# Strassen's seven products for part of the FFN down projection, woven between gate and up chunks

## The chip, the cores and the metric

The kernel runs on one core of a Trainium2 chip. The metric is the device time of one execution in microseconds. A core has a matrix engine (TensorE: PE in the profile, its weight loads PEld), VectorE (DVE), ScalarE (ACT), GpSimd (POOL) and SyncE (SP, which issues most DMAs here). The engines run side by side, each works through its own list in order, and they wait for each other by semaphores. PE multiplies a stationary block of 128x128 with a moving block of 128 rows and up to 512 columns into a bank of the accumulator memory (PSUM); DVE and ACT carry the sums out of it.

## What is computed

Two decoder layers over 512 tokens of width 1024, all in float32. Layer 0 mixes tokens by sliding-window attention, layer 1 by a chunked spatial gating unit (SGU). Each ends with the FFN that the change touches:

```
def swiglu(h, w_gate_up, w_down):
    gu = h @ w_gate_up                                   # 1024 -> 2 x 2816
    return (silu(gu[..., :2816]) * gu[..., 2816:]) @ w_down   # 2816 -> 1024
...
h = rmsnorm(x, norm_ffn_pre[i])
x = x + rmsnorm(swiglu(h, ...), norm_ffn_post[i])
```

## The kernel before

**Precision by three products.** Every float32 operand is split into a high part that the matrix engine takes at full rate (float32r, hi) and the rest (lo). `mm3` (line 210) issues hi·hi, hi·lo and lo·hi, so each block of a projection costs three matmuls. Activations are split once, where they are made; weights are split as they stream in.

**Weight stream.** All weights lie in HBM in the order of use, in chunks of eight 128x128 blocks (512 KB). `fetch` (223) issues the load of a chunk into one of `NRAW` = 2 raw buffers through SyncE's queue. `split` (238) makes the chunk ready: ACT copies raw to the high tile `wh` (257), DVE subtracts to the low tile `wl` (253). High and low tiles come from one pool of `NW` = 17 tiles of 128x1024; rows of gains and biases (`row_tile`) take tiles of it too. A chunk gives its two tiles back when its last use is issued.

**Order by a planner.** The lists of PE, DVE and ACT are written out when the program is built. A planner keeps a modelled time `now` for PE and busy times for DVE and ACT; `Side` objects are generators of follow-up steps with due times (softmax, evacuations, norms). `tick` (155) runs what is due and otherwise asks `split_idle` (262) whether the next chunk should be split: at once if its slack is below a stage's bound (`PLAN`), else only if ACT and DVE are free and no step marked as a chain is due soon.

**FFN before (609).** The 22 slices of 128 hidden columns go in two halves of 11 (`HJ`). A half makes gate and up for its slices: per slice two PSUM banks, eight k blocks, 48 matmuls of 512 columns and two chunks. The first three slices of the first half run by token halves with 256 columns, because tokens 2 and 3 are not normalised yet. `evac_gu` (610) takes a slice out: ACT's Silu (614), DVE's product with the up half (620), ACT's high part (624), DVE's low part (627). The half's down projection then runs over its 11 slices: for each of the two column halves and four token blocks, `tok_mm` (590) adds three matmuls of 512 columns per slice. The first half's sums are copied to tiles `m` by ACT (678); the second half's are added to them by DVE (689) and start each token's norm (`Tok`, 488). In the last FFN the last token's second column half runs as two of 256 columns, and its results are written out (567).

**Around it.** Attention comes before the first FFN, SGU before the second. At each boundary the weights of the next stage are split ahead as far as `NW` tiles allow, while DVE and ACT run the norm of the tokens.

Of the kernel before, what the change touches and what calls it, by code (L numbers as in the profile page):

```python
# [6 lines left out]
F32 = mybir.dt.float32  # L7
# [13 lines left out]
HJ = NJ // 2  # L21
# [4 lines left out]
NW = 17  # L26
# [5 lines left out]
NRAW = 2  # L32
# [16 lines left out]

V0 = 0  # L50
# [5 lines left out]
SV0 = GU0 + 3 * NJ * KT  # L56
# [5 lines left out]
NBLK = GU1 + 3 * NJ * KT  # L62

def uses(i):

    if i < Q0 or WO0 <= i < GU0 or SO0 <= i < GU1:
        return 4
    if SV0 <= i < SO0:  # L70
        return 4 if i < SU0 or SV1 <= i < SU1 else 2 if i < SV1 else 1
    if i < WO0:
        return 1
    b = i - GU0 if i < SV0 else i - GU1
    f, b = divmod(b, 3 * HJ * KT)
    if b >= 2 * HJ * KT:
        return 4
    return 2 if f == 0 and b < 3 * 2 * KT else 1
# [3 lines left out]
def trunk_kernel(ctx, tc, x_t, xt, w, cols, rows, ws_t, consts, out):  # L82
# [136 lines left out]
    left = [0] * NCH  # L219
    for i in range(NBLK):  # L220
        left[i // CB] += uses(i)

    def fetch(free=0.0, most=NBLK):
        while len(raws) < min(NCH, len(chunks) + NRAW, most):
            c = len(raws)
            if c == NLATE:
                load_x()
            if c == NLATE + 1:
                nc.sync.dma_start(c_msk[:, 0:256], consts[:, 1024:1280])
                nc.sync.dma_start(c_msk[:, 256:384], consts[:, 1408:1536])  # L230
                nc.sync.dma_start(cs[:], consts[:, 0:1024])
                busy["d"] += 2.5
            raw = rawp.tile([P, CB * P], F32, tag="raw", name=nm("raw"))
            nc.sync.dma_start(raw[:], w[c])
            busy["d"] = max(busy["d"], now[0], free) + 1.46
            raws[c] = (raw, busy["d"] + DLAT)

    def split():
        c = len(chunks)
        fetch()  # L240
        raw, ready = raws[c]
        assert used[0] + 2 <= NW
        used[0] += 2
        wh = wp.tile([P, CB * P], F32R, tag="w", name=nm("wh"))
        wl = wp.tile([P, CB * P], F32R, tag="w", name=nm("wl"))

        def low(f):
            yield f
            if c in POOL_LOW:
                nc.gpsimd.tensor_tensor(wl[:], raw[:], wh[:].bitcast(F32), ALU.subtract)  # L250
                chunks[c][3] = f + 2.4
            else:
                nc.vector.tensor_tensor(wl[:], raw[:], wh[:].bitcast(F32), ALU.subtract)  # L253
                chunks[c][3] = V(CB * P, f)
            fetch(chunks[c][3])

        nc.scalar.activation(wh[:], raw[:], AF.Copy)  # L257
# [52 lines left out]
    def drop(n=1):  # L310
        used[0] -= n

# [296 lines left out]
    def ffn(base, nx_in, g1o, nx_out):  # L609
# [30 lines left out]

        h = hsrc(nx_in)

        def gu(g, b0, j, hf):
            grab("acc")
            grab("acc")
            ps = (acc(), acc())
            for k in range(KT):
                rh, rl = h(k, hf)
                for u in range(2):
                    wh, wl = blk(b0 + (j * KT + k) * 2 + u)  # L650
                    mm3(ps[u][:, hf], wh, wl, rh, rl, k == 0, k == KT - 1)
                tick()
            evac_gu(g, j, *ps, hf)

        m = None
        for f in range(2):
            stage[0] = (2 if base == GU0 else 6) + f
            b0 = base + f * (HJ * KT * 3)
            ga = [gp.tile([P, 8, S], F32R, tag="ga", name=nm("ga")) for _ in range(2)]
            gb = [gp.tile([P, 3, S], F32R, tag="gb", name=nm("gb")) for _ in range(2)]  # L660
            g = [[ga[i][:, k] if k < 8 else gb[i][:, k - 8] for k in range(HJ)] for i in range(2)] + [{}]
            j0 = 0
            if f == 0:
                pace[0] = 2.5
                for hf in halves:
                    for j in range(3):
                        gu(g, b0, j, hf)
                j0 = 3
            pace[0] = 5.1
            for j in range(j0, HJ):  # L670
                gu(g, b0, j, full)
            d0 = b0 + HJ * KT * 2
            l = gsrc(g)
            if f == 0:
                m = new_m()
                for c in range(2):
                    def evac0(t, ps):
                        nc.scalar.activation(m[t][c][:], ps[:], AF.Copy)
                        A(S, now[0] + 0.2)
                    tok_proj(d0 + c * HJ * 4, HJ, l, evac0)  # L680
                continue
# [10 lines left out]
            tok_proj(d0, HJ, l, lambda t, ps: add(t, 0, ps), False)  # L692
            hold[0] = now[0] + NB * HJ * 0.65
            for t in range(NB if nx_out is not None else NB - 1):
                grab("acc")
                ps = acc()
                for k in range(HJ):
                    tok_mm(ps, l, t, k, d0 + HJ * 4 + 4 * k, k == 0, k == HJ - 1)
                add(t, 1, ps)
            if nx_out is None:  # L700
                t = NB - 1
                until(lambda: toks[0].done)
                for i, hf in enumerate(halves):
                    grab("acc")
                    ps = acc()[:, 0:256]
                    for k in range(HJ):
                        lh, ll = l(k, slice(t * P, (t + 1) * P))
                        wh, wl = blk(d0 + HJ * 4 + 4 * k, 4 if i else 0, 4)
                        mm3(ps, lh, ll, wh[:, hf], wl[:, hf], k == 0, k == HJ - 1)
# [3 lines left out]
            drop()  # L713


    def attention(nx_in, g1o, nx_out):
# [263 lines left out]
        hold[0] = now[0] + NB * 8 * 0.65 + 10  # L980
        for t in range(NB):
            tok = Tok(t, m[t], g1, nx_out)
            for c in range(2):
# [7 lines left out]
        drop(2)  # L991


    def sgu(nx_in, g1o, nx_out):
# [157 lines left out]
        drop()  # L1152
# [73 lines left out]
def _layout(inputs):  # L1226
# [30 lines left out]
    def ffn(i):  # L1257
        gu = blocks(a["ffn_w_gate_up"][i]).reshape(KT, 2, NJ, P, P)
        dn = blocks(a["ffn_w_down"][i])
        for h in range(2):  # L1260
            js = slice(h * HJ, (h + 1) * HJ)
            seq.append(gu[:, :, js].transpose(2, 0, 1, 3, 4).reshape(-1, P, P))
            for c in range(2):
                seq.append(flat(dn[js][:, 4 * c:4 * c + 4]))
# [12 lines left out]
    assert w.shape[0] == NBLK  # L1277
    w = np.ascontiguousarray(w.reshape(NBLK // CB, CB, P, P).transpose(0, 2, 1, 3).reshape(NBLK // CB, P, CB * P))

# [40 lines left out]
```

## Time and profile before

| | |
|---|---|
| median of 3 runs | 1066.5 us (1066.02 to 1067.13) |
| the profiled execution | 1067.36 us |
| its span, first to last instruction | 1065.6 us |
| PE busy | 1046.0 us, 98% |
| DVE busy | 524.8 us, 49% |
| ACT busy | 438.4 us, 41% |
| moved by DMA | 105.10 MB, 99 GB/s over the span |
| mean granted clock of PE | 0.994 |

The profiled execution lies 1.8 us above its own span. PE's ends are modelled in this profile, so its busy time overlaps from one matmul to the next; the distance from start to start tells the rate, and the wait for another engine tells a stall.

### The profile page before, as it was taken

Reading aid. Unit: us, or ns where it says so; the run is one execution under the profiler, and the core shown is the slowest. Engines: PE = TensorE matmul, PEld = TensorE weight load, DVE = VectorE, ACT = ScalarE, POOL = GpSimd, SP = SyncE. Lnnn points to the kernel's source line nnn. Section 1 sums busy time; section 2 is a strip of 40 time slices with the busy share of each in tenths; the row PEclk is TensorE's granted clock in tenths of the full one; section 3 lists DMA queues with packets and bytes.
Section 4 is the critical chain, followed back from the end, with each engine's and each line's share of the span. In section 5 each row is a group of like instructions: output and inputs, shape, how many; then the busy total and the mean of one; then the engine's idle time right before and its main releaser. Section 6 shows DMA issues by size and latency. Waiting matters only on the chain.

```text
span 1065.6 us, 13311 instructions
## 1 busy us (share of the span) xinstructions
PE 1046.0 (98%) x5237; PEld 869.6 (82%) x5237; DVE 524.8 (49%) x1074; ACT 438.4 (41%) x775; POOL 24.2 (2%) x22
## 2 busy tenths in 40 slices
PE   7998998999999999999999999999999999999997
PEld 6875666988888888888889888899888888888886
DVE  6699679743332233332474867584333223333335
ACT  4799676632322223222255444573223222232210
POOL 2000002000000000000000000100000000000000
PEclk9999999999999999999999999999999999999999
DMA  8322101433233322223133233034223332222302
GB/s 292 125 93 80 60 21 60 131 127 99 99 99 99 99 99 95 94 92 135 59 119 100 79 125 106 28 120 151 90 97 98 99 99 99 99 99 98 101 1 80
DMA packets 29839, 105.10 MB, mean 99 GB/s; under 512 B 3344, under 2 KB 3872, under 8 KB 29776
## 3 DMA queue, kind: packets, MB, share of 16 engines
q1 hardware_dynamic: 29088, 103.10, 29.1%
q8 instruction: 41, 0.67, 0.3%
q10 hardware_dynamic: 576, 0.92, 0.2%
q0 software_dynamic: 112, 0.23, 0.2%
q14 instruction: 22, 0.18, 0.0%
HBM read 102.13 MB, written 2.10 MB: 98 GB/s over the span
## 4 chain that ended last, share of the span: by engine, by line
PE 88%; DVE 7%; ACT 2%; DMA 1%; issue 1%; POOL 0%; DVEq 0%; ACTq 0%; POOLq 0%
PE acc L204 86%; DVE wl L253 1%; DVE p L828 1%; ACT rt L746 1%; PE aux L459 1%; DVE p L859 1%; DMA raw<-w 1%; PE acc L888 1%; DMA c_cols<-cols 1%; PE aux L896 0%; DVE rt L740 0%; ACT wh L257 0%; ACT p L850 0%; DVE hl L1168 0%; PE aux L457 0%
## 5 line engine op out<-in xcount | busy, mean ns | idle before, releaser
L253 DVE TENSOR_TENSOR wl<-raw,wh 128x1024 fp32r<-128x1024 f32 x174 | 214.5, 1234 | 413.0 <-PE acc L204 340.4
L204 PE MATMUL acc<-hh,wh 128*128 128x512 f32 (+1 forms) x960 | 352.1, 367 | 0.0
L204 PE MATMUL acc<-hl,wh 128*128 128x512 f32 (+1 forms) x960 | 349.8, 364 | 0.0
L204 PE MATMUL acc<-hh,wl 128*128 128x512 f32 (+1 forms) x960 | 349.7, 364 | 0.0
L257 ACT ACTIVATE wh<-raw 128x1024 fp32r<-128x1024 f32 x176 | 185.8, 1058 | 220.4 <-PE acc L204 184.6
L204 PE MATMUL acc<-wh,ga 128*128 128x512 f32 (+1 forms) x736 | 236.2, 392 | 2.7 <-DVE ga L915 2.7
L204 PEld LDWEIGHTS acc<-hh,wh 128*128 128x128 f32 x960 | 181.0, 188 | 29.1 <-issue 0.2
L204 PEld LDWEIGHTS acc<-hh,wl 128*128 128x128 f32 x960 | 180.9, 188 | 28.9
L204 PEld LDWEIGHTS acc<-hl,wh 128*128 128x128 f32 x960 | 181.0, 189 | 28.8 <-issue 0.2
L204 PEld LDWEIGHTS acc<-wh,ga 128*128 128x128 f32 x736 | 138.3, 189 | 35.1 <-issue 4.9
L204 PE MATMUL acc<-wl,ga 128*128 128x512 f32 (+1 forms) x368 | 142.3, 387 | 0.0
L614 ACT ACTIVATE t<-acc 128x512 f32<-128x512 f32 (+1 forms) x50 | 27.3, 545 | 146.5 <-PE acc L204 146.5
L204 PEld LDWEIGHTS acc<-wl,ga 128*128 128x128 f32 x368 | 69.8, 190 | 12.8
L204 PE MATMUL acc<-wh,gb 128*128 128x512 f32 (+1 forms) x198 | 61.9, 383 | 0.0
L624 ACT ACTIVATE ga<-t 128x512 fp32r<-128x512 f32 (+1 forms) x38 | 21.5, 565 | 53.5 <-DVE t L620 53.4
L204 PEld LDWEIGHTS acc<-wh,gb 128*128 128x128 f32 x198 | 36.9, 188 | 7.2
L503 POOL TENSOR_TENSOR m<-m,row 128x512 f32<-128x512 f32 x12 | 17.2, 1433 | 1020.6 <-ACT acc L381 1020.6
L204 PE MATMUL acc<-wh,hh 128*128 128x512 f32 (+1 forms) x96 | 34.4, 368 | 4.4 <-ACT wh L257 4.4
L204 PE MATMUL acc<-wl,gb 128*128 128x512 f32 (+1 forms) x99 | 37.9, 383 | 0.0
L381 ACT ACTIVATE acc<-m 128x512 f32<-128x512 f32 x30 | 18.0, 598 | 46.5 <-DVE m L689 42.1
L204 PE MATMUL acc<-wh,hl 128*128 128x512 f32 (+1 forms) x96 | 34.3, 367 | 0.7 <-DVE hl L1168 0.7
L627 DVE TENSOR_TENSOR ga<-t,ga 128x512 fp32r<-128x512 f32 (+1 forms) x38 | 23.1, 607 | 21.1 <-ACT ga L624 21.1
(124 smaller groups left out, 830.4 us busy)
## 6 DMA issues: line engine op xcount, KB each, us to landing
raw<-w SPq DMA_DIRECT2D x176, 512.0 KB, 3.5
row<-rows SPq DMA_DIRECT2D x8, 512.0 KB, 4.5
xg<-xt SPq DMA_DIRECT2D x4, 512.0 KB, 7.3
x<-x_t SPq DMA_DIRECT2D x4, 512.0 KB, 7.3
out<-x SPq DMA_DIRECT2D x4, 256.0 KB, 2.1
out<-x ACTq DMA_DIRECT2D x3, 256.0 KB, 2.1
cs<-consts SPq DMA_DIRECT2D x1, 512.0 KB, 7.2
t<-ws_t SPq DMA_DIRECT2D x2, 256.0 KB, 4.3
```

What stands on the lines that cost most here:

```text
L204: nc.tensor.matmul(ps, a, b, start=start, stop=stop)
L253: nc.vector.tensor_tensor(wl[:], raw[:], wh[:].bitcast(F32), ALU.subtract)
L257: nc.scalar.activation(wh[:], raw[:], AF.Copy)
L381: nc.scalar.activation(junk, src, AF.Square, accum_out=s[:, c:c + 1])
L459: nc.tensor.transpose(dst, self.src[t][k // 4][:, (k % 4) * P:(k % 4 + 1) * P], ident)
L503: nc.gpsimd.tensor_tensor(self.m[c][:], self.m[c][:], self.g1[:, cols2[c]], ALU.mult)
L614: nc.scalar.activation(t1[:, hf], pg[:, hf], AF.Silu)
L624: nc.scalar.activation(g[0][jj][:, hf], t1[:, hf], AF.Copy)
L627: nc.vector.tensor_tensor(g[1][jj][:, hf], t1[:, hf], g[0][jj][:, hf].bitcast(F32), ALU.subtract)
L746: nc.scalar.activation(ro[o:o + 32, hf], t1[q * 32:q * 32 + 32, hf], AF.Identity, bias=b[q * 32:q * 32 + 32])
L828: nc.vector.tensor_tensor_reduce(pt[:, 2 * g2 + g, i, 0:nk], sc[i][:, g * 256:g * 256 + nk], mask[:, 256 - nk:256], 0.125, sink_bc[:, pr * ...
L859: nc.vector.tensor_scalar(p(j), p(j), sm[:, j:j + 1], None, ALU.mult)
```

## The change

The down projection of the first 12 of the 22 slices (`AJ`) is no longer done as a plain product. Its operand is cut into token halves (two of 256), slices of a pair (even and odd) and column halves (two of 512), which makes it a 2x2 by 2x2 block product, and that is done by Strassen's seven products instead of eight. Each product sums over three groups of four slices (`NQ`) and keeps two PSUM banks; `settle` copies or adds its sums into the tiles `m`, 24 times in all per FFN.

The left operand of a product is a sum or difference of two blocks of the activations (five of seven products) or one block (two of seven), made by DVE and then split by ACT and DVE into a ring of two (`operands`). The right one is a sum or difference of two weight chunks (again five of seven): both are loaded, DVE adds or subtracts one into the other, then the sum is split as any chunk. A chunk of weights is loaded and split anew for each product that takes it.

The first 12 slices' gate and up come first, with their activations kept unsplit in float32 (`evac_raw`: Silu and product only). Then 21 product steps (7 products, 3 groups, 12 matmuls each) and 20 half slices of gate and up of the other ten slices (24 matmuls each) alternate: one half slice, two product steps, then one and one. The plain down projection of those ten slices ends the FFN as before. Besides: `NW` falls from 17 to 15, `NRAW` rises from 2 to 4, and a gain row's tile counts as free only when the tokens have used it (`drop_after`).

```
-NW = 17
+NW = 15
-NRAW = 2
+NRAW = 4
+AJ = 12
+BJ = NJ - AJ
+NQ = AJ // 4
...
+PRODUCTS = (
+    (((0, 0), (1, 1), 1), ((0, 0), (1, 1), 1)),
+    (((1, 0), (0, 0), -1), ((0, 0), (0, 1), 1)),
+    (((1, 1), None, 0), ((1, 0), (0, 0), -1)),
+    (((0, 1), (1, 1), -1), ((1, 0), (1, 1), 1)),
+    (((0, 0), None, 0), ((0, 1), (1, 1), -1)),
+    (((0, 0), (0, 1), 1), ((1, 1), None, 0)),
+    (((1, 0), (1, 1), 1), ((0, 0), None, 0)),
+)
...
     def fetch(free=0.0, most=NBLK):
-        while len(raws) < min(NCH, len(chunks) + NRAW, most):
+        while len(raws) < min(NCH, most) and raw_used[0] + len(STREAM[len(raws)][0]) <= NRAW:
...
+        if len(tiles) == 2:
+            op = ALU.add if STREAM[c][1] > 0 else ALU.subtract
+            nc.vector.tensor_tensor(raw[:], raw[:], tiles[1][:], op)
+            f = V(CB * P, ready)
+            raw_used[0] -= 1
+            fetch(f)
+            chunks[c] = [wh, wl, None, None, f]
+            chunks[c][2] = Side(high_low(f), f)
+            return
...
-        slack = max(now[0], hold[0]) + (c - cur[0] - 1) * pace[0] - max(now[0], busy["v"], busy["a"]) - 2.4
+        slack = max(now[0], hold[0]) + (c - cur[0] - 1) * pace[0] - max(now[0], busy["v"], busy["a"]) - (2.4 if len(STREAM[c][0]) == 1 else 3.7)
...
+                if y is not None:
+                    yield from take("t")
+                    t = tmp()[:].rearrange("p (a t) -> p a t", a=2)
+                    nc.vector.tensor_tensor(t, src, view(y), ALU.add if sign > 0 else ALU.subtract)
+                    src = t
+                    f = V(S, now[0])
+                    yield f
+                hi, lo = (r.rearrange("p (a t) -> p a t", a=2) for r in ring[n % 2])
+                nc.scalar.activation(hi, src, AF.Copy)
+                f = A(S, f)
+                yield f
+                nc.vector.tensor_tensor(lo, src, hi.bitcast(F32), ALU.subtract)
...
+        Side(operands(), now[0], True)
+        pace[0] = 4.0
...
+        def settle(p, ps):
+            for sign, th, c in TARGETS[p]:
+                for i in range(2):
+                    d = m[2 * th + i][c][:]
+                    if sign == "=":
+                        nc.scalar.activation(d, ps[i][:], AF.Copy)
+                        A(S, now[0] + 0.2)
+                    else:
+                        nc.vector.tensor_tensor(d, d, ps[i][:], ALU.add if sign == "+" else ALU.subtract)
+                        V(S, now[0] + 0.2)
+
+        for kind, a, b in ITEMS:
+            if kind == "g":
+                if b == 0:
+                    gps = two()
+                gu(gps, at - b * CB, range(4 * b, 4 * b + 4), full)
+                if b:
+                    evac_gu(g, a - AJ, *gps, full)
+            else:
+                if b == 0:
+                    banks = two()
+                until(lambda: (a, b) in made)
+                f, hi, lo = made[a, b]
+                wait(f)
+                for kp in range(2):
+                    for i in range(2):
+                        ts = slice(i * P, i * P + P)
+                        wh, wl = blk(at + 4 * kp, 4)
+                        mm3(banks[i][:], hi[:, kp, ts], lo[:, kp, ts], wh, wl,
+                            b + kp == 0, b == NQ - 1 and kp == 1)
+                        tick()
+                spent[0] += 1
+                if b == NQ - 1:
+                    settle(a, banks)
```

## Rows read from the trace of the kernel before

**Rows 1.** The page's first part: the span, and each engine's busy us, share and instructions.

```profile
span 1065.6 us, 13311 instructions
PE 1046.0 (98%) x5237; PEld 869.6 (82%) x5237; DVE 524.8 (49%) x1074; ACT 438.4 (41%) x775; POOL 24.2 (2%) x22
```

**Rows 2.** What PE waited for over the whole span: all rows of that view (engine, line, releaser: us in total, times, longest us).

```profile
PE acc L204 <- ACT wh L257: 4.4, 1, 4.4
PE aux L896 <- ACT t L900: 3.6, 3, 2.4
PE acc L204 <- DVE ga L915: 2.7, 1, 2.7
PE acc L172 <- DVE zero L164: 1.1, 1, 1.1
PE acc L204 <- DVE hl L1168: 0.7, 1, 0.7
```

**Rows 3.** The chain that ended last, in order of time (start us, us, what): its two longest pieces, one in each FFN.

```profile
205.46 336.82 PE acc L204 x1548
...
714.43 344.14 PE acc L204 x1617
```

**Rows 4.** The list of PE's instructions in order of time (start us, us shown, line, operation): matmuls of 512 columns in a row, in the first half's gate and up and then in its down projection; then, at the start of the first FFN, matmuls of 256 columns.

```profile
300.04 0.39 PE L204 MATMUL acc<-hh,wh 128*128 128x512 f32 x1
300.27 0.39 PE L204 MATMUL acc<-hl,wh 128*128 128x512 f32 x1
...
302.31 0.39 PE L204 MATMUL acc<-hl,wh 128*128 128x512 f32 x1
...
329.74 0.39 PE L204 MATMUL acc<-wh,ga 128*128 128x512 f32 x1
329.96 0.39 PE L204 MATMUL acc<-wh,gb 128*128 128x512 f32 x1
...
183.09 0.28 PE L204 MATMUL acc<-hh,wh 128*128 128x256 f32 x1
...
183.67 0.28 PE L204 MATMUL acc<-hh,wl 128*128 128x256 f32 x1
```

**Rows 5.** Busy time by stretch of 20 us: the stretch, its length, then busy us (instructions) of PE, PEld, DVE, ACT, POOL, then PE's granted clock, the DMA share and GB/s. Attention (60:80, 80:100), its end and the first FFN's start (160:180), the first FFN's gate and up (440:460), SGU (600:620), the second FFN's start (720:740).

```profile
60.00:80.00 20.00, 20.00 (x121) 14.94 (x120) 19.48 (x62) 19.16 (x51) 0.00 (x0) 1.00 0.25 79
80.00:100.00 20.00, 18.02 (x101) 12.30 (x99) 18.86 (x58) 19.76 (x42) 0.00 (x0) 1.00 0.23 80
...
160.00:180.00 20.00, 17.33 (x78) 12.41 (x77) 19.53 (x55) 11.22 (x25) 5.49 (x4) 0.91 0.17 54
...
440.00:460.00 20.00, 20.00 (x90) 16.57 (x89) 6.28 (x8) 5.46 (x8) 0.00 (x0) 1.00 0.32 106
...
600.00:620.00 20.00, 20.00 (x90) 16.57 (x89) 19.40 (x45) 8.78 (x13) 0.00 (x0) 1.00 0.16 53
...
720.00:740.00 20.00, 20.00 (x136) 18.54 (x135) 9.63 (x12) 8.42 (x12) 0.00 (x0) 1.00 0.49 163
```

**Rows 6.** Groups of instructions by line with different shapes kept apart (line, engine, operation, names, shapes, count | busy us, mean ns of one | idle us of the engine before them and who ended it).

```profile
L253 DVE TENSOR_TENSOR wl<-raw,wh 128x1024 fp32r<-128x1024 f32 x174 | 214.5, 1234 | 413.0 <-PE acc L204 340.4 <-ACT wh L257 72.3
L257 ACT ACTIVATE wh<-raw 128x1024 fp32r<-128x1024 f32 x176 | 185.8, 1058 | 220.4 <-PE acc L204 184.6 <-DMA raw<-w 35.6
...
L620 DVE TENSOR_TENSOR t<-t,acc 128x512 f32<-128x512 f32 x38 | 25.8, 680 | 0.0
...
L614 ACT ACTIVATE t<-acc 128x512 f32<-128x512 f32 x38 | 22.8, 599 | 142.0 <-PE acc L204 142.0
...
L627 DVE TENSOR_TENSOR ga<-t,ga 128x512 fp32r<-128x512 f32 x26 | 18.0, 693 | 18.2 <-ACT ga L624 18.2
...
L624 ACT ACTIVATE ga<-t 128x512 fp32r<-128x512 f32 x26 | 16.5, 633 | 45.1 <-DVE t L620 45.1
...
L689 DVE TENSOR_TENSOR m<-acc,m 128x512 f32<-128x512 f32 x15 | 10.0, 688 | 24.3 <-PE acc L204 24.3
L678 ACT ACTIVATE m<-acc 128x512 f32<-128x512 f32 x16 | 9.6, 598 | 15.7 <-PE acc L204 14.7
...
L751 DVE TENSOR_TENSOR rt<-rt,cs 128x512 f32<-128x512 f32 x10 | 6.8, 685 | 0.0
```

**Rows 7.** The page's last part, the loads of weights: queue, count, KB each, median us from issue to landing.

```profile
raw<-w SPq DMA_DIRECT2D x176, 512.0 KB, 3.5
```

**Rows 8.** Who waited for whom on SyncE's queue in the first 60 us, and ACT's list in the same stretch: the wait of the third chunk's split for its load.

```profile
SPq L234 <- POOL wl L250: 8.0, 2, 6.4
...
17.57 1.06 ACT L257 ACTIVATE wh<-raw 128x1024 fp32r<-128x1024 f32 x1 [3.12 <-DMA raw<-w]
```

**Rows 9.** DVE's list in order of time at the three stage boundaries: the third chunk of the first FFN; the last chunks split before the second FFN and the next; token 1's last add before SGU and the low part of the last of its activation blocks.

```profile
177.92 1.22 DVE L253 TENSOR_TENSOR wl<-raw,wh 128x1024 fp32r<-128x1024 f32 x1
...
665.84 1.23 DVE L253 TENSOR_TENSOR wl<-raw,wh 128x1024 fp32r<-128x1024 f32 x1 [0.26 <-ACT wh L257]
697.03 1.23 DVE L253 TENSOR_TENSOR wl<-raw,wh 128x1024 fp32r<-128x1024 f32 x1 [1.21 <-ACT wh L257]
...
532.80 0.69 DVE L689 TENSOR_TENSOR m<-acc,m 128x512 f32<-128x512 f32 x1 [2.70 <-PE acc L204]
...
551.49 0.87 DVE L476 SCALAR_TENSOR_TENSOR hl<-aux,c_cols,hh 128x256 fp32r<-128x256 f32 x2
```

More of the change, by code (lines that the diff above doesn't have):

```diff
@@ L20 @@
 NJ = FF // P
-HJ = NJ // 2
 EPS = 1e-6
@@ L48, with _items, _stream, plain @@
 GROUPS = ((0,), (1,), (2, 3))
+PRODUCTS = (
[7 rows of a table added]
+)
+TARGETS = (
+    (("=", 0, 0), ("=", 1, 1)),
+    (("+", 1, 1),),
+    (("=", 1, 0), ("+", 0, 0)),
+    (("+", 0, 0),),
+    (("=", 0, 1), ("+", 1, 1)),
+    (("+", 0, 1), ("-", 0, 0)),
+    (("+", 1, 0), ("-", 1, 1)),
+)
+def _items():
+    ps = [("p", p, q) for p in range(len(PRODUCTS)) for q in range(NQ)]
+    gs = [("g", AJ + j, half) for j in range(BJ) for half in range(2)]
+    n, out = len(ps) + len(gs), []
+    while ps or gs:
+        if gs and (not ps or len(gs) * (n - len(gs)) >= len(ps) * len(gs) and len(gs) >= len(ps) * BJ * 2 / (7 * NQ)):
+            out.append(gs.pop(0))
+        else:
+            out.append(ps.pop(0))
+    return out
+ITEMS = _items()
+def _stream():
+    st, n = [], [0]
+    def plain(blocks, uses):
+        for _ in range(blocks // CB):
+            st.append(((n[0],), 0, uses))
+            n[0] += 1
+    def ffn():
+        plain(3 * 2 * KT, 2)
+        plain((AJ - 3) * 2 * KT, 1)
+        gb = n[0]
+        qb = gb + 2 * BJ
+        for kind, a, b in ITEMS:
+            if kind == "g":
+                st.append(((gb + 2 * (a - AJ) + b,), 0, 1))
+            else:
+                x, y, sign = PRODUCTS[a][1]
+                at = lambda z: qb + 4 * b + 2 * z[0] + z[1]
+                st.append(((at(x),) if y is None else (at(x), at(y)), sign, 2))
+        n[0] = qb + 4 * NQ
+        plain(2 * BJ * 4, 4)
+    plain(16, 4)
+    plain(80, 1)
+    plain(64, 4)
+    ffn()
+    plain(32, 4)
+    plain(16, 2)
+    plain(32, 4)
+    plain(48, 1)
+    plain(64, 4)
+    ffn()
+    return st, n[0]
+STREAM, NHBM = _stream()
 V0 = 0
@@ L232, in fetch @@
                 busy["d"] += 2.5
[L233 to L236, printed above, removed]
+            tiles = []
+            for b in reversed(STREAM[c][0]):
+                raw = rawp.tile([P, CB * P], F32, tag="raw", name=nm("raw"))
+                nc.sync.dma_start(raw[:], w[b])
+                busy["d"] = max(busy["d"], now[0], free) + 1.46
+                tiles.insert(0, raw)
+            raw_used[0] += len(tiles)
+            raws[c] = (tiles, busy["d"] + DLAT)
     def split():
@@ L240, in split @@
         fetch()
-        raw, ready = raws[c]
+        tiles, ready = raws[c]
+        raw = tiles[0]
         assert used[0] + 2 <= NW
@@ L311, in drop, with drop_after, side @@
         used[0] -= n
+    def drop_after(toks):
+        def side():
+            while any(len(t.half) < 2 for t in toks):
+                yield now[0] + 0.2
+            drop()
+        Side(side(), now[0])
     xs = [xp.tile([P, D], F32, tag=f"x{k}", name=f"x{k}") for k in range(NB)]
@@ L644, in gu, with two @@
+        h = hsrc(nx_in)
+        def gu(ps, b, js, hf):
+            for k in js:
+                rh, rl = h(k, hf)
+                for u in range(2):
+                    wh, wl = blk(b + 2 * k + u)
+                    mm3(ps[u][:, hf], wh, wl, rh, rl, k == 0, k == KT - 1)
+                tick()
+        def two():
             grab("acc")
             grab("acc")
[L646 to L678, printed above, removed]
-                        A(S, now[0] + 0.2)
-                    tok_proj(d0 + c * HJ * 4, HJ, l, evac0)
-                continue
+            return acc(), acc()
@@ new lines, in pair_tile @@
+        def pair_tile(dt=F32):
+            grab("rt")
+            return tp.tile([P, 2, S], dt, tag="rt", name=nm("rt"), bufs=3)
+        stage[0] = 2 if base == GU0 else 6
+        pace[0] = 2.5
+        for hf in halves:
+            for j in range(3):
+                ps = two()
+                gu(ps, base + j * 2 * KT, range(KT), hf)
+                evac_raw(raw_g(j), j, *ps, hf, raw_ready)
+        pace[0] = 5.1
+        for j in range(3, AJ):
+            if j == 8:
+                rt += [pair_tile(), pair_tile()]
+            ps = two()
+            gu(ps, base + j * 2 * KT, range(KT), full)
+            evac_raw(raw_g(j), j, *ps, full, raw_ready)
@@ L682, in ffn @@
+        for _ in range(3):
+            give("rt")
+        pace[0] = 5.1
+        stage[0] += 1
+        d0 = at
+        l = gsrc(g)
+        if 1:
             spare[0] = 0
@@ L1151, in sgu @@
             evac(t, 1, ps)
-        drop()
+        drop_after(toks)
+        for _ in range(NY):
+            give("rt")
     n0, n1, n2, n3 = (NextH(i) for i in range(4))
```

123 lines of the change are left out of this document (89 added, 34 removed).

## Prediction

> **What bounds the kernel now.** I read the page's engine table first: PE is busy in 98% of the span, DVE in 49%, ACT in 41% [rows 1]. Because PE's ends are modelled, I then asked what PE waited for: five waits in the whole span, 12.5 us together, all on lines of the start and of attention and none on a line of the FFN [rows 2]. The chain that ended last says the same: one piece of matmuls runs for 336.8 us through the first FFN and one for 344.1 us through the second [rows 3]. The last question is the rate. Ten matmuls of 512 columns start between 300.04 and 302.31, so 0.227 us from one to the next, and the rows of the down projection show the same step [rows 4]. A stretch of 20 us at granted clock 1.00 holds about 90 of them, in gate and up with DVE at 6.28 us and in SGU with DVE at 19.40 us alike [rows 5]. So in the FFN the time is the number of matmuls times 0.227 us, whatever DVE and ACT do, as long as operands are ready.
>
> **What is removed.** A plain projection of 12 slices takes 12 x 4 token blocks x 2 column halves x 3 = 288 matmuls of 512 columns. Seven products in three groups of 12 matmuls take 252. That is 36 fewer per FFN and 72 in all; the other matmuls stay (the last token's few of 256 columns shift by 0.03 us). 72 x 0.227 = 16.3 us, all of it on PE's path: **-16.3 us**.
>
> The Trainium skill's page "TensorE: Matmul & The Clock Gate", section "Back-to-back issue gap", gives about 131 ns per matmul of 512 columns for a sustained stream and 216 ns for the isolated gap. By the first this term would be 9.4 us and by the second 15.5 us. The trace sides with neither exactly: 0.227 us is far above the first and 11 ns above the second, and here the rows decide.
>
> **What is added, and whether it hides.** The new work lies in a stretch of 21 product steps and 20 half slices, 21 x 12 + 20 x 24 = 732 matmuls or 166.2 us of PE per FFN. From the durations in [rows 6], DVE has there: 41 low parts of chunks at 1.234 us (50.6); 15 sums of two raw chunks, a form the trace lacks, taken like the low part because both add two 128x1024 operands (18.5); 15 sums of activations like the 0.685 us of L751 (10.3); 21 low parts of these at 0.693 (14.6); 16 additions from PSUM into `m` at 0.688 (11.0); ten slices' product and low part at 0.680 and 0.693 (13.7). Sum 118.7 us, 71% of the stretch. ACT has 41 high parts at 1.058 (43.4), 21 at 0.633 (13.3), 8 copies at 0.598 (4.8), ten Silus and high parts at 0.599 and 0.633 (12.3): 73.8 us, 44%. The loads are 36 for the products and 20 for the halves, 56 of 0.524 MB or 29.4 MB in 166.2 us: 177 GB/s. At 163 GB/s, with half of PE's work at 256 columns, PE had no gap [rows 5].
>
> An average isn't enough, so take one period, a half slice and a product step: 36 matmuls, 8.17 us. The heaviest kind on DVE is a product with sums on both sides: 1.23 for the half slice's chunk, 2.47 for the pair, 1.38 for the operand, 1.37 where a slice is finished, 1.38 where the product's two additions fall: 7.8 us. The last two products have four additions (2.75) but no pair to add: 1.23 + 1.23 + 1.38 + 1.37 + 2.75 = 8.0. Both fit, barely. A pair needs 1.23 + 1.06 + 1.23 = 3.5 us from landing to ready. The operand chain is alive through the whole stretch and marked as a chain, so the planner splits there only when slack is below its bound, 2.0 us in the first FFN: chunk c starts about when chunk c-2 is begun, one period ahead of use. Loads need 3.5 us [rows 7], and with four raw buffers one pair and two halves' worth are on the way. So there is a margin of 2 to 4 us, larger in the second FFN (bound 10.0). The ring of two operands has its next refill two product steps ahead, which is over 8 us for some 2 us of work.
>
> What can get late is a chunk's low part on DVE behind the additions of `settle`, which stand in DVE's list until PE ends the product, with the queued low parts behind them and PE waiting for those. Low end 0 (below zero is excluded, PE has no wait there to lose); high end one low part, 1.23 us, at each of 14 product ends, 17 us. I take **+1.5 us**, near the low end, because DVE at 19.40 us of 20 cost PE nothing in SGU [rows 5], and that is a denser stretch.
>
> Elsewhere on the path: the first 12 slices lose ACT's and DVE's splitting, and the copies of the first half (16 at 0.598 us, 8 per FFN) stay 8 per FFN; none was on the path.
>
> **The boundaries.** Two weight tiles fewer mean one chunk less split ahead. At the first FFN the third chunk was low-split at 177.92; the first matmul of that FFN starts at 183.09 and a chunk lasts 24 x 0.116 = 2.8 us there [rows 4, 9], so the third is needed at about 188.7 and may come 9 us later. Before the second FFN nothing was split between 665.84 and 697.03 [rows 9]: the tiles were full, and now one of those chunks falls into the norm's stretch. Before SGU each of the last two tokens' columns shrinks by 0.68 us, so token 1's norm, added at 532.80 and done at 552.4 [rows 9], has 1.4 us less. Bounds 0 to 3 x 1.23 + 1.4 = 5 us; I take **+0.5 us**, since the first and third have spare time. `drop_after` only tells the planner of a wait that the tile had anyway.
>
> **The start.** Four raw buffers instead of two let loads go out earlier: SyncE's queue waited 8.0 us for GpSimd's low parts to free a raw buffer, and ACT 3.12 us for the third chunk [rows 8]. PE was not waiting for that chunk; from 60 to 100 us DVE and ACT are the full engines (19.48 and 19.16, 18.86 and 19.76 of 20) [rows 5], and their work is the same in another order, with fewer chunks split ahead. A reordered list can gain or lose the 2 to 3 us of a wait as in [rows 2]. Bounds -4 to +4, I take **0**.
>
> **The sum.** The profiled execution of before took 1067.36 us, 1.8 above its span. 1067.36 - 16.3 + 1.5 + 0.5 + 0 = 1053.1. It is 0.86 above the median of the runs, so the median of after should be 1052.2; I say **1052**.
>
> **The rivals.** *Prefetch lost (1055 to 1062 us, 12%).* The chunk less at the boundaries and attention's reordered lists cost their upper bounds, 5 + 4 us, above the main case. For it: 160 to 180 us, where DVE is busy for 19.53 us and PE lost 2.7 us to a DVE operation with two low parts near it. Against: the spare times above.
>
> *A lighter start (1046 to 1049, 10%).* The earlier loads pull attention's work forward and its waits shrink by up to 4 us, with no cost in the stretch.
>
> *DVE and ACT set the stretch's pace (about 1100, 6%; the slower side).* If steps that hand over between the two wait in line so that the engines hardly overlap, a period takes the sum of both: 2.29 (half's chunk) + 3.17 (product's chunk, with 5/7 of the sum) + 1.82 (operand) + 1.30 (half an evacuation) + 0.75 (settling) = 9.33 us against PE's 8.17. 41 periods in both FFNs x 1.16 = 48 us, so 1100. It decides from 16.3 / 41 = 0.40 us per period on, at 8.57 us. For it: DVE's low parts have 72.3 us of idle time ended by ACT's high part [rows 6]. Against: with 19.48 and 19.16 us of 20 the two do overlap in attention, and here 71% and 44% ask for little.
>
> *It doesn't do what it says (1066, 2%).* A wait of PE at each of the 42 product steps of 0.39 us would eat the gain; PE's steps show no such gaps now.
>
> **How the numbers follow.** Main case 70% (1049 to 1055), the rivals as given. The range 1048 to 1058 takes in the main case, most of the lighter start and the lower part of lost prefetch, and leaves out some 17%. About 0.2%, 2.1 us, is what a measurement of this kernel can tell from no change, so "faster" means below 1064.4: 70 + 12 + 10 less a little, 0.91; same 0.03; slower 0.06.
>
> **What would show it.** Right: 72 fewer matmuls of 512 columns, their steps still 0.227 us; DVE near 71% and ACT near 44% in the stretch, DMA near 177 GB/s; hardly any wait of PE on a low part `wl` or the operand's `lo`. Wrong: waits of PE on L253's successor or on the raw sum (the pace rival); gaps of PE before the first matmuls of an FFN or of SGU (lost prefetch); a longer step between matmuls at the higher load; or attention ending later or earlier than its 183 us by more than 2.

## The result, and the profile after

The changed kernel takes **1060.42 us** (median of 4 runs, 1059.17 to 1060.86) against 1066.82 (4 runs, 1066.02 to 1067.44) for the kernel before: a ratio of 0.9939, 95% interval 0.9921 to 0.9956. It is 6.4 us faster. The forecast was 1052, 14.5 us faster, with a range that ended at 1058. The profiled execution of after took 1060.68 us.

The page's first part, beside [rows 1]:

```profile
span 1058.7 us, 13445 instructions
PE 1033.2 (98%) x5162; PEld 856.6 (81%) x5162; DVE 628.0 (59%) x1196; ACT 461.8 (44%) x805; POOL 23.8 (2%) x22
```

PE's share tells nothing: it is 98% in both. So I cut the span at the first matmul of each stage in the list of PE's instructions. These are the four rows of after (start us, us shown, line, operation): the first FFN's gate, SGU, the second FFN's gate, and the last matmul of the kernel:

```profile
192.06 0.28 PE L269 MATMUL acc<-hh,wh 128*128 128x256 f32 x1
...
549.77 0.39 PE L269 MATMUL acc<-wh,hh 128*128 128x512 f32 x1
...
696.53 0.28 PE L269 MATMUL acc<-hh,wh 128*128 128x256 f32 x1
...
1051.43 0.28 PE L269 MATMUL acc<-wh,gb 128*128 128x256 f32 x1
```

The first of the same four in the kernel before lies at 183.09 [rows 4], and these are the other three:

```profile
549.34 0.48 PE L204 MATMUL acc<-wh,hh 128*128 128x512 f32 x1
...
695.25 0.28 PE L204 MATMUL acc<-hh,wh 128*128 128x256 f32 x1
...
1058.28 0.28 PE L204 MATMUL acc<-wh,gb 128*128 128x256 f32 x1
```

The differences:

| stage (to the next one's first matmul) | before | after | difference |
|---|---|---|---|
| attention | 183.09 | 192.06 | **+8.97** |
| first FFN | 366.25 | 357.71 | **-8.54** |
| SGU | 145.91 | 146.76 | +0.85 |
| second FFN | 363.03 | 354.90 | **-8.13** |

Both FFNs give what the removed matmuls promised. More than half of it is lost again in attention, whose code the change doesn't touch. The second FFN's gain is kept to the end.

The busy time by stretch shows both sides. The columns are those of [rows 5]: first, of after, the whole stretch of product steps and half slices in each FFN; then the time from 60 us to the first FFN, in before and in after:

```profile
331.00:497.00 166.00, 166.00 (x734) 137.47 (x733) 105.50 (x123) 68.81 (x89) 0.00 (x0) 1.00 0.53 168
834.00:1000.00 166.00, 166.00 (x734) 137.45 (x733) 105.33 (x123) 68.41 (x89) 0.00 (x0) 1.00 0.51 166
...
60.00:183.09 123.09, 116.83 (x649) 81.51 (x648) 105.22 (x346) 95.07 (x256) 5.49 (x4) 0.97 0.18 61
...
60.00:192.06 132.06, 120.90 (x646) 83.03 (x644) 105.43 (x343) 93.97 (x253) 5.36 (x4) 0.95 0.17 57
```

In the stretch PE issues 734 matmuls in 166 us, 0.226 us each, at granted clock 1.00, while DVE is busy for 64%, ACT for 41%, and DMA moves 168 GB/s. In attention DVE and ACT do the same work in both kernels (105 and 94 to 95 us); it only takes longer.

What PE waited for over the whole span of after, the view of [rows 2]:

```profile
PE acc L1093 <- ACT t L1105: 6.6, 3, 3.8
PE acc L269 <- ACT wh L341: 3.8, 1, 3.8
PE acc L269 <- DVE ga L1120: 3.0, 2, 2.6
PE acc L269 <- DVE hl L1378: 2.1, 2, 1.4
PE acc L237 <- DVE zero L229: 1.1, 1, 1.1
PE aux L1101 <- ACT t L1105: 0.9, 2, 0.6
PE acc L269 <- ACT ga L1115: 0.7, 1, 0.7
PE acc L269 <- DVE hl L568: 0.4, 1, 0.4
```

No row names a low part of a weight chunk or a product's operand: the new work in the FFN makes PE wait nowhere. What grew is attention's wait for `t`, the copy of the transposed probabilities (L1105 here, L900 before): 3.6 us in [rows 2], 6.6 + 0.9 = 7.5 here.

The longest of these, 3.78 us, shows how such a wait arises. PE's list of after, then ACT's list in the same 6 us:

```profile
94.51 1.07 PE L1093 MATMUL acc<-t,vt 128*64 128x512 f32 x2
99.37 0.84 PE L1093 MATMUL acc<-t,vt 128*64 128x512 f32 x1 [3.78 <-ACT t L1105]
```

```profile
94.32 1.04 ACT L341 ACTIVATE wh<-raw 128x1024 fp32r<-128x1024 f32 x1
95.39 2.91 ACT L951 ACTIVATE rt<-rt,c_cols 32x512 f32<-32x512 f32 x4
98.33 0.51 ACT L1068 ACTIVATE p<-p,sm 128x256 f32<-128x256 f32 x1
98.74 0.58 ACT L1105 ACTIVATE t<-aux 128x512 f32<-128x512 f32 x1
```

ACT is never idle here. PE waits because a chunk's high part (1.04 us) and four rope steps (2.91 us) stand ahead of the copy in ACT's list. The copy took no longer than it did (590 ns on average in both); the lists are in another order.

PE issues the same 932 matmuls ahead of the first FFN in both kernels, with the same count of each shape, so attention's +8.97 us is time lost and no work. Waits make 4.9 us of it: from 60 us to the first FFN they were 6.3 us in 4 places (3.6 + 2.7, [rows 2]) and are now 11.2 in 8 (6.6 + 3.0 + 0.9 + 0.7). The other 4.1 us are longer steps between matmuls that wait for nothing. The lower clock level accounts for some 3 us of these at most: a granted clock of 0.97 over 123.09 us is 3.7 us less of full clock in before, and 0.95 over 132.06 us is 6.6 us less in after. The last section shows such a stretch.

### The profile page after: what moved, and what is told of

The parts are those of the page before. It is cut to its first block, busy times and chain, and to the rows that moved or that the text cites. A ratio compares the mean times of both kernels' runs of the same rounds, so it can differ in the third digit from the quotient of the medians.

```text
span 1058.7 us, 13445 instructions
## 1 busy us (share of the span) xinstructions
PE 1033.2 (98%) x5162; PEld 856.6 (81%) x5162; DVE 628.0 (59%) x1196; ACT 461.8 (44%) x805; POOL 23.8 (2%) x22
## 5 line engine op out<-in xcount | busy, mean ns | idle before, releaser
L322 DVE TENSOR_TENSOR wl<-raw,wh 128x1024 fp32r<-128x1024 f32 x192 | 235.4, 1231 | 228.8 <-PE acc L269 91.2
L341 ACT ACTIVATE wh<-raw 128x1024 fp32r<-128x1024 f32 x164 | 170.7, 1054 | 114.4 <-PE acc L269 107.8
L269 PE MATMUL acc<-wh,ga 128*128 128x512 f32 (+1 forms) x480 | 157.1, 394 | 3.6 <-DVE ga L1120 3.0
L269 PEld LDWEIGHTS acc<-wh,ga 128*128 128x128 f32 x480 | 90.2, 190 | 25.7 <-DVE ga L1120 3.8
L269 PE MATMUL acc<-wl,ga 128*128 128x512 f32 (+1 forms) x240 | 92.6, 386 | 0.0
L269 PE MATMUL acc<-wh,gb 128*128 128x512 f32 (+1 forms) x244 | 79.5, 386 | 0.0
L269 PE MATMUL acc<-wh,rt 128*128 128x512 f32 x208 | 68.5, 390 | 0.0
L329 ACT ACTIVATE wh<-raw 128x1024 fp32r<-128x1024 f32 x30 | 31.7, 1058 | 67.6 <-DVE raw L334 67.6
L269 PEld LDWEIGHTS acc<-wl,ga 128*128 128x128 f32 x240 | 45.7, 190 | 7.8
L269 PEld LDWEIGHTS acc<-wh,rt 128*128 128x128 f32 x208 | 39.0, 188 | 8.1
L269 PE MATMUL acc<-wl,rt 128*128 128x512 f32 x104 | 40.5, 389 | 0.0
(143 smaller groups left out, 1050.7 us busy)
```

What stands on the lines that cost most here:

```text
L269: nc.tensor.matmul(ps, a, b, start=start, stop=stop)
```

## The experiments

**Theory A.** The planner writes the lists of all engines from the number of weight tiles and raw buffers. With 15 tiles and four raw buffers it writes other lists for attention; their order costs 9 us, and the stretch costs nothing.
**Theory B.** Fewer chunks lie ready at the stage boundaries (the prefetch that is lost).
**Theory C.** Gain and loss both belong to the stretch: its DVE and ACT work holds something up.

### The old buffers under the new FFN: e1_stretch_big_pool

```diff
-NW = 15
+NW = 17
-NRAW = 4
+NRAW = 2
```

> The kernel after with NW 17 and NRAW 2, as before: attention's lists are then instruction for instruction those of before, and the Strassen stretch has only two raw buffers. Theory A (the loss sits in attention, made by the two buffer counts): the first FFN starts near 183.1 us as before and not at 192.1, the matmuls saved stay saved, about 1066.8 - 16.3 + 0.7 (what SGU lost) = 1051 us plus whatever two raw buffers cost the stretch. A pair then can't load before the chunk ahead of it is split: 3.5 us of load and 3.5 us of making it, 7.0 us against a period of 8.2, so 0 to 10 us over both FFNs. Theory B (the loss is made by the stretch itself and only shows early): the first FFN still starts near 192 us and the time stays near 1060.

Measured: 1097.68 us (1096.93 to 1098.94), ratio 1.0296 (1.0281 to 1.0312). Attention ends at 181.34, so the 9 us are gone from there; but the two FFNs take 386.57 and 374.85 us, 28.9 and 20.0 more than in after, where the expectation allowed 10 at most. What PE waited for, two rows that after does not have:

```profile
PE acc L269 <- ACT wh L329: 13.9, 16, 2.4
PE acc L269 <- DVE wl L322: 13.2, 19, 0.8
```

With two raw buffers a pair of chunks fills the ring, and no load can go ahead. The waits are 27.1 us, the loss 48.8. PE's list of this run shows part of the other 21.7; these are two places with the same two waits:

```profile
371.50 0.49 PE L269 MATMUL acc<-wh,gb 128*128 128x512 f32 x1 [0.95 <-ACT wh L329]
372.76 0.50 PE L269 MATMUL acc<-wl,gb 128*128 128x512 f32 x1 [0.76 <-DVE wl L322]
...
373.56 0.39 PE L269 MATMUL acc<-wl,gb 128*128 128x512 f32 x1
373.79 0.63 PE L269 MATMUL acc<-wh,gb 128*128 128x512 f32 x2
...
392.90 0.49 PE L269 MATMUL acc<-wh,gb 128*128 128x512 f32 x1 [0.95 <-ACT wh L329]
394.16 0.50 PE L269 MATMUL acc<-wl,gb 128*128 128x512 f32 x1 [0.76 <-DVE wl L322]
...
395.12 0.63 PE L269 MATMUL acc<-wl,gb 128*128 128x512 f32 x1
395.54 1.05 PE L269 MATMUL acc<-wh,gb 128*128 128x512 f32 x2
```

After the first pair of waits matmuls start 0.23 us apart as ever (373.56 and 373.79); after the second, 0.42 us apart (395.12 and 395.54), about half the rate. Summed over PE's list of both FFNs, the 39 steps at the lower clock level cost 7.3 us. Another 7.4 us lie in the 35 steps with the waits themselves, mostly because a wait is counted from the modelled end of the matmul before it, 0.39 us after its start, where the step is 0.227 us. The remaining 7 us were not followed. So the four raw buffers are needed in the FFN, and attention's time follows tiles and raw buffers, not the FFN.

### The new buffers under the old FFN: e3_plain_small_pool and e4_plain_fewer_tiles

The kernel before, with `drop_after`, and 15 tiles; e3 has four raw buffers as well (`NRAW = 4`), e4 keeps two. (e9 below has no `drop_after`, and its attention lists are those of e4, so `drop_after` plays no part there.)

```diff
-NW = 17
+NW = 15
...
-            drop()
+            if nx_out is not None:
+                drop_after(toks)
...
-        drop(2)
+        drop()
+        drop_after(toks)
```

> The kernel before, with the plain down projection, but NW 15, NRAW 4 and drop_after: attention's lists are those of after. Theory A: the first FFN starts near 192.1 us and the whole takes 9 us more than before, about 1076 us (1074 to 1078). Theory B: 1067, since there is no Strassen stretch to cost anything.

> The kernel before with NW 15 alone (and drop_after, which changes no instruction), NRAW 2: parts theory A. If the chunk fewer split ahead makes the loss (A1), the first FFN starts near 192 us and the time is about 1076. If the earlier loads by four raw buffers and the other order that the planner makes of them do (A2), it starts near 183 us and the time stays within 2 us of 1067. Anything between shares it.

Measured: e3 1075.87 us (ratio 1.0088, 1.0071 to 1.0105), e4 1072.71 (1.0058, 1.0043 to 1.0073). The plain kernel gets slower by what after loses: the first FFN starts at 192.44 in e3, where attention's lists are those of after (192.06), and at 188.78 in e4. So two tiles fewer cost 5.7 us and two raw buffers more another 3.7; starts of equal lists differ by up to 2.0 us (see e9), so the split between the two is no surer than that. The FFNs take 365.90 and 363.10 us in e3, 365.90 and 363.01 in e4. That prices the change of the FFN alone: 365.90 - 357.71 = 8.19 and 363.10 - 354.90 = 8.20, together 16.39 us. Theory C falls.

### Both buffers in turn: e2_lent_raws and e5_two_raws_in_attention

e2 has 17 tiles and two raw buffers, and while pairs of chunks are ahead up to two loads go into free weight tiles. e5 is after with two raw buffers until attention's end.

```diff
...
+    def room(n):
+        need = n - min(n, NRAW - raw_used[0])
+        pairs = any(len(s[0]) == 2 for s in STREAM[len(raws):len(raws) + 4])
+        return not need or pairs and len(lent) + need <= 2 and used[0] + need + 2 <= NW
...
-                raw = rawp.tile([P, CB * P], F32, tag="raw", name=nm("raw"))
+                if raw_used[0] < NRAW:
+                    raw = rawp.tile([P, CB * P], F32, tag="raw", name=nm("raw"))
+                    raw_used[0] += 1
+                else:
+                    raw = wp.tile([P, CB * P], F32, tag="w", name=nm("raw"))
...
```

```diff
-        while len(raws) < min(NCH, most) and raw_used[0] + len(STREAM[len(raws)][0]) <= NRAW:
+        while len(raws) < min(NCH, most) and raw_used[0] + len(STREAM[len(raws)][0]) <= (2 if stage[0] < 2 else NRAW):
```

> The kernel after with NW 17 and NRAW 2, where the stretch takes up to two more raw buffers from the pool of weight tiles while pairs are ahead and gives them back. Attention's lists are those of before. Theory A: the first FFN starts near 183.1 us, no wait of PE in the stretch, 1051 us (1049 to 1053). Theory B: the first FFN starts near 192 us, about 1060.

> The kernel after, with only two raw buffers used until the first FFN begins: attention's lists are those of the plain kernel with 15 tiles and two raw buffers, whose first FFN started at 188.8 us. If the two counts add up, the first FFN starts at 188.8 +- 1 and the whole takes about 1060.4 - 3.3 = 1057 us. If the Strassen stretch loses something by this (its first chunks come with fewer raws ahead), it stays at 1060.

Measured: e2 **1049.92 us** (1048.32 to 1050.17), ratio 0.9844 (0.9829 to 0.9859); e5 1056.86 (one run). In e2 the first FFN starts at 182.33 and the FFNs take 357.74 and 354.80 us, those of after. Its attention has the lists of before, and PE's waits are those of before again:

```profile
PE acc L269 <- ACT wh L359: 3.7, 1, 3.7
PE aux L1120 <- ACT t L1124: 3.5, 3, 2.4
PE acc L269 <- DVE ga L1139: 2.7, 1, 2.7
```

So both gains can be had together: 16.6 us below before (1066.49 in the runs beside it), 10.5 below after. e5 takes the raw buffers' share out and starts the FFN at 188.15, as e4 did at 188.78; their attention lists are the same.

### One wait's cause, one suspected engine, one boundary: e6, e7, e8

e6 raises the planner's time of a rope step on ACT (modelled 0.57 us, measured 0.72), so that it places the copies truer. e7 puts the low parts of chunks 18 and 19 on GpSimd, in case DVE is what attention lacks. e8 lets the planner split chunks in that stage only when slack is below 2.0 us instead of 6.0, to see whether an early split in the way is the cost.

```diff
-                    f = A(n, f, 0.14)
+                    f = A(n, f, 0.30)
```

> The kernel after, with the planner's time for each of ACT's four rotary steps raised from 0.57 to 0.73 us, what the trace shows (4 steps in 2.92 us). Theory P: the lists are written for an ACT that is quicker than it is, so PE's list puts the products of values ahead of other work and PE stands for the copy on ACT (3.8 us at 94.5 us and 2.6 at 147.5); then the first wait goes and the first FFN starts 2 to 4 us earlier, near 189, total about 1057. Rival Q: the fewer tiles push two splits into a full stretch, whatever the list assumes; then it starts within 1 us of 192 and the total stays near 1060.

```diff
-POOL_LOW = (0, 1)
+POOL_LOW = (0, 1, 18, 19)
```

> The kernel after, with the low parts of the last two attention chunks (those that fewer tiles push from 121 us and before to 137 and 152) on GpSimd instead of DVE. If DVE's 2 x 1.23 us there make the loss (Q on DVE), the first FFN starts 2 to 4 us earlier, near 189, total near 1057. If it is ACT's high parts or PE's order (P), it starts within 1 us of 192.

In e8 the first number of `PLAN`'s second entry falls from 6.0 to 2.0; only that entry is shown:

```diff
-(6.0, 0.8, 0.0, (3,), (1, 2))
+(2.0, 0.8, 0.0, (3,), (1, 2))
```

> The kernel after, with the planner's slack bound in the attention output stage lowered from 6.0 to 2.0 us, so that chunks are split there only when nearly due or when ACT and DVE are free. If the place of ACT's high part ahead of the values' copy at 149.6 us makes PE's wait at 147.5 (P), that wait shrinks from 2.6 by about 1 us and the first FFN starts 1 to 3 us earlier. If splits come too late instead, PE waits on wl there and it starts later than 192. Q alone gives no change, within 1 us.

Measured, one run each: e6 1056.21, e7 1063.17, e8 1060.15. In e6 the two longest waits of after for `t` (3.78 and 2.58 us) are gone and the FFN starts at 187.50, but another wait took their place, one row of its list of PE's waits:

```profile
PE acc L269 <- DVE ga L1120: 7.6, 2, 4.9
```

In e7 the FFN starts later, at 196.24 (and takes 1.8 us less), which neither side expected. It does not settle whether DVE's capacity is the cause, because DVE was not relieved. While GpSimd made the two low parts (134.93 to 137.32 and 151.88 to 154.23), operations of DVE took longer: one on 128x4 numbers took 2.21 us, and the three of the second row here 3.00 us, where the same three took 0.88 us at 137.85. The two low parts would have cost DVE 2.4 us:

```profile
135.13 2.21 DVE L1040 TENSOR_TENSOR es<-c_row,st 128x4 f32<-128x4 f32 x1
...
151.91 3.00 DVE L1064 TENSOR_SCALAR p<-p,sm 128x256 f32<-128x256 f32 x3
```

e7 also has a wait that after lacks: 5.4 us before the transposes of the FFN's operand (L549). What speaks against DVE's capacity is e10 below, where the work is the same and only its order differs.

In e8 the first FFN starts at 186.85, 5.2 us earlier, and takes 4.8 us longer. Two rows of PE's list:

```profile
159.92 0.50 PE L269 MATMUL acc<-wl,ga 128*128 128x512 f32 x1 [1.65 <-DVE wl L322]
...
189.97 0.39 PE L269 MATMUL acc<-hl,wh 128*128 128x256 f32 x1 [2.76 <-DVE hl L568]
```

The first lies in attention's output projection, a chunk split too late, and is the longer of two such waits there (2.4 us together). The second is the FFN's own: after one matmul at 186.85 PE stands for `hl`, the low part of the normalised operand, which DVE made only after the low part of a chunk (188.31 to 189.53). So the earlier start is one matmul, and no wait in the FFN is for a chunk. SGU starts at 549.36 against 549.77: nothing won. A chunk that comes too late, theory B's kind of cost, shows only in attention's own projection here, where splits are held back on purpose.

### Order alone: e9_one_chunk_later and e10_plain_truer_rope

The lists of e4 are those of before up to the split of chunk 18. There the pool of 15 tiles is full, and the split waits. e9 is the kernel before, with 17 tiles, but with the cap of 15 for that chunk alone. e10 is the kernel before with only e6's planner time: no buffer, load or operation differs, only their order.

```diff
-        if c >= NCH or used[0] + 2 + spare[0] > NW or (c and not chunks[c - 1][2].done):
+        if c >= NCH or used[0] + 2 + spare[0] > (15 if c == 18 else NW) or (c and not chunks[c - 1][2].done):
```

> The kernel before with one thing changed: while chunk 18 is the next to be split, the pool counts as 15 weight tiles instead of 17, so that this one chunk's split moves back by some 14 us and the steps behind it in the lists of ACT and DVE are reordered; every other chunk sees 17 tiles. Theory A (the loss in attention comes through the order of the lists, set off by the first chunk that finds no tiles): the first FFN starts near 188.8 us as in the plain kernel with 15 tiles, not at 183.1, and the run takes about 1072. Theory B (the loss comes from having fewer chunks ready at the end of attention): the tiles of the end are all there, so the first FFN starts at 183 to 184 and the run takes 1066 to 1067.

```diff
-                    f = A(n, f, 0.14)
+                    f = A(n, f, 0.30)
```

> The kernel before with only the planner's modelled time of a rope step on ACT changed (0.30 us more overhead instead of 0.14, nearer to the measured 0.72): no buffer, no load and no arithmetic differs, only the order of the lists. Theory A (the order of attention's lists by itself is worth several us in either direction): the start of the first FFN moves by more than 1.5 us from 183.1, either way, and the time with it. Theory B (the order is worth little, the buffers cost the time): 182 to 184.5, and 1066 to 1067. If truer times are what helps, as 187.5 against 192.1 in the changed kernel suggested, it starts at 179 to 181 and takes about 1063.

Measured, one run each, before at 1067.05 (7 runs) beside them: e9 1071.0, e10 1076.52. e9's low parts stand in DVE's list at these times (the first two rows: chunks 17 and 18), and below them the same two of before:

```profile
116.17 1.22 DVE L253 TENSOR_TENSOR wl<-raw,wh 128x1024 fp32r<-128x1024 f32 x1
133.28 1.22 DVE L253 TENSOR_TENSOR wl<-raw,wh 128x1024 fp32r<-128x1024 f32 x1
...
118.07 1.22 DVE L253 TENSOR_TENSOR wl<-raw,wh 128x1024 fp32r<-128x1024 f32 x1
...
120.80 1.22 DVE L253 TENSOR_TENSOR wl<-raw,wh 128x1024 fp32r<-128x1024 f32 x1
```

Chunk 18 comes 17.1 us after chunk 17; in before it was 2.7 us after (118.07 and 120.80). From chunk 17's low part, up to which the lists are the same, to the first FFN's first matmul: before 65.0 us (183.09 - 118.07), e9 70.6 (186.79 - 116.17), e4 70.8 (188.78 - 117.97). The lists of PE, DVE, ACT and GpSimd in e9 are those of e4, instruction for instruction, up to the first FFN. So this one displaced chunk, with what it pushes about, is the whole cost of the two tiles. The absolute starts differ more, by up to 2.0 us where the lists are equal (186.79 and 188.78 in e9 and e4; 181.34, 182.33 and 183.09 in e1, e2 and before), which is why I count from chunk 17.

Theory B falls by a count: when the first FFN's first matmul starts, the low parts of 23 chunks are done in before, in after and in each of e1 to e11. With 15 tiles no chunk was missing there. Ahead of the second FFN the count is equal too (112 with the old FFN, 121 with the new). Only ahead of SGU is one chunk fewer ready with 15 tiles (97 in after against 98 in e2, 88 in e4 against 89 in before), and there SGU takes 0.5 and 0.2 us longer (146.76 against 146.26, 146.13 against 145.91).

e10 is the plainest case. Its first FFN starts at 192.33, 9.2 us late, with the buffers of before. The busy time of the slice from 80 us (columns as in [rows 5]), and PE's list in it:

```profile
80.00:100.00 20.00, 14.25 (x72) 10.21 (x70) 19.48 (x62) 18.15 (x46) 0.00 (x0) 0.83 0.22 79
```

```profile
94.11 1.22 PE L204 MATMUL acc<-wh,ga 128*128 128x512 f32 x2 [4.63 <-DVE ga L915]
95.12 0.63 PE L204 MATMUL acc<-wl,ga 128*128 128x512 f32 x1
95.55 1.05 PE L204 MATMUL acc<-wh,ga 128*128 128x512 f32 x2
```

In [rows 5] the same slice held 101 matmuls; here it holds 72, with DVE as full as ever (19.48 us). One wait of 4.63 us, then 0.43 us from matmul to matmul. PE issues the same 932 matmuls ahead of the first FFN as in before. Order alone is worth 9 us.

### Is a truer planner better? e11_lent_raws_truer_rope

e2 with e6's planner time.

```diff
-                    f = A(n, f, 0.14)
+                    f = A(n, f, 0.30)
```

> The kernel of the lent raw buffers (17 weight tiles, two raw buffers, up to two more lent from the weight tiles while pairs of chunks are ahead) with the rope step's modelled time raised from 0.14 to 0.30 us of overhead. Theory A (order is chance as far as the planner goes): the first FFN starts anywhere within 4 us of 182.3, and the time is 1046 to 1054 with the two FFNs and SGU unchanged at 357.7, 146.3 and 354.8 us. Theory B (truer times take waits away in general): the first FFN starts near 178 and the time is about 1045.5.

Measured: 1060.13 us (1058.25 to 1060.59), ratio 0.9926 (0.991 to 0.9943): 10.2 us slower than e2. The FFN starts at 192.03, as in e10, and its longest wait, 4.6 us for `ga`, is e10's:

```profile
PE acc L269 <- DVE ga L1139: 7.6, 3, 4.6
```

The FFNs are unchanged at 357.72 and 354.80. That is outside even theory A's band: the FFN starts 9.7 us from 182.3 where 4 were allowed, and 1060.13 lies above 1054. A truer time helped after (e6: 187.50 against 192.06) and harmed before and e2 by 9 to 10 us. So it is no rule that truer times help: the lists differ by several us however they come about.

## Why the prediction was wrong

One reading on the way was loose, without effect on the sum: [rows 2] holds five rows, but seven waits.

**Removed matmuls (-16.3): right.** 16.39 us measured, on equal surroundings (e3 against after).

**The stretch (+1.5): too high, with the right mechanism.** 72 x 0.227 is 16.34 us and 16.39 were measured, so the stretch cost nothing. DVE was busy for 105.5 us where 118.7 were counted, ACT for 68.8 against 73.8, and the loads ran at 168 GB/s against 177. The sum of two raw chunks, which the trace of before lacks, took 1.22 us as the low part did; it is the row of L334, from the groups with shapes kept apart:

```profile
L334 DVE TENSOR_TENSOR raw<-raw,raw 128x1024 f32<-128x1024 f32 x30 | 36.6, 1219 | 0.0
```

The additions of `settle` held no low part up so long that PE waited. The pace rival fell with this, and with it the slower side; e1 shows the condition: four raw buffers. With two, the stretch costs 49 us.

**The boundaries (+0.5): right in size, in part by luck.** -6.85 in all from first matmuls to last, less +8.97 and -16.39, leaves +0.57. But the premise, one chunk less split ahead, held only before SGU, where it came with 0.5 us (e9); at both FFNs as many chunks were ready as before. PE's wait of 0.38 us on `hl`, 5.5 us into SGU, is the part foreseen for token 1's norm.

**The start and attention (0, bounds -4 to +4): this step failed.** It measured +8.97. The prediction saw that the lists would be reordered and then priced that as one wait of [rows 2], 2 to 3 us, won or lost alike, with bounds of -4 and +4. Both the size and the balance were wrong. First, a displaced chunk does not move one wait: it moves the split, and with it the copies, rope steps and norms that share ACT and DVE; the places where PE waits went from 4 to 8. Some of these waits also have a price beyond themselves, since PE then runs at half rate for a while. Second, the two directions were not alike: the list of before had only 6.3 us of such waits, and all six other lists tried for this stage (one shared by e4, e5 and e9, one by after and e3, one by e10 and e11) ended it later than 183.1 us: e6 and e8 by 4 (e8 then paid in the FFN), e9 by 4 or, counted from chunk 17, by 6, e4 and e5 by 5 to 6, after, e3, e10 and e11 by 9, e7 by 13 (with GpSimd's part in it). None went the other way; that better lists exist is not excluded.

The rival "prefetch lost" gave 1055 to 1062 and named attention's reordered lists among its causes, so the time falls there. Its first cause, fewer chunks ready, was not the mechanism (23 were ready in both); its second was, at more than twice its price, and 12% was too little for it. The forecast's own sum without the attention term agrees with e2: 1049.92, where the sum less the stretch's 1.5 us says 1050.7.

**What the signs were.** "Hardly any wait of PE on `wl` or `lo`" and "DVE near 71%, ACT near 44%" came out on the side of the forecast; "attention ending later than its 183 us by more than 2" was named as a sign against it, and is what happened.

**Still open.** Why the raw buffers' part of the order costs its 3 to 4 us (e4 to e3, after to e5) was not followed to one instruction as the tiles' part was to chunk 18. No experiment looked for an order better than that of before, and none relieved DVE or ACT in attention without changing the order.

## What to carry to other kernels

Where a planner writes the instruction lists, a buffer count is not a local constant: it rewrites the order of stages that the change doesn't touch, so price those stages by their own spread, measured by a change of order alone (as e10), before summing. Compare the lists first: if an untouched stage has another list, expect its time to move, by 4 to 9 us in a stage of 183 us here. And where a stage needs more buffers only for a while, lend them there (e2) and leave the rest of the lists alone.

## What was not expected of the hardware

A wait can cost PE more than its length. At the end of after's attention, PE's list and then the stretch by itself (columns as in [rows 5]):

```profile
182.20 1.22 PE L269 MATMUL acc<-wh,ga 128*128 128x512 f32 x2 [2.60 <-DVE ga L1120]
183.22 0.63 PE L269 MATMUL acc<-wl,ga 128*128 128x512 f32 x1
183.65 1.06 PE L269 MATMUL acc<-wh,ga 128*128 128x512 f32 x2
184.50 0.63 PE L269 MATMUL acc<-wl,ga 128*128 128x512 f32 x1
```

```profile
182.20:186.60 4.40, 4.40 (x10) 3.51 (x11) 4.33 (x23) 1.05 (x2) 1.29 (x1) 0.50 0.28 112
```

After a wait of 2.60 us three matmuls take 1.28 us (183.22 to 184.50), 0.43 us each against 0.227 at other times, and the granted clock of these 4.4 us is 0.50: the lower of the clock's two levels, 1.2 GHz. It is no fixed price per wait: in e1 two waits of 0.95 and 0.76 us were followed by this step at 392.90 and not at 371.50. Over e1's FFNs 27.1 us of waits came with 48.8 us of loss, of which the steps at the lower level are 7.3.

The Trainium skill's page "TensorE: Matmul & The Clock Gate", in Part 1 under "Wait — 56ns, not 53.3ns?", gives 426.7 ns from start to start at 512 columns on the lower level and 215.7 on the upper. The traces agree with the first (0.43 us) and lie 11 ns above the second (0.227 us).
